# Squares of the last attention's queries on ScalarE, and 64 bytes of padding in SBUF

## The chip, the core and the metric

The kernel runs on one core of a Trainium2 chip. The metric is the device time of one execution in microseconds. Before the change it is 1250.59 us, the median of three runs (1250.11 to 1250.6).

## What is computed

Two transformer blocks in a row on 256 tokens of width 1024, in float32. The first block mixes with a spatial gate, a forgetting attention and a cross attention, and has a feed-forward part with 4096 inner columns (squared ReLU). The second has two layers; each is a SwiGLU feed-forward part of 2816 inner columns, an attention, and another such part: a sliding-window attention in the first layer, a latent attention in the second. The change touches the latent attention:

```python
q = (rmsnorm_2(c_q, q_norm) @ w_uq).reshape(B, S, B_HEADS, dqk)      # 16 heads of 96
k = jnp.concatenate([k_nope, broadcast(k_rope)], axis=-1)
q = rmsnorm_2(q, q_gain); k = rmsnorm_2(k, k_gain)
q = concat(q[..., :64], apply_rope(q[..., 64:], pos))
s = einsum('bqhd,bshd->bhqs', q_blk, k) * dqk**-0.5;  p = softmax(causal(s));  o = p @ v
```

The norm of `q` needs, for each token and head, the sum of the squares of 96 numbers.

## The kernel before

**Products.** The weights come from HBM in pieces (`Stream`, L73): a tile `raw`, three of them in turn, is cast by ScalarE to `wh` in the format fp32r (L103), and VectorE writes the remainder `wl` = `raw` − `wh` (L113); six pairs of `wh` and `wl` are in turn. The low part of a piece also issues the next DMA, on SP's queue. Activations are held as such pairs too: `xh`, `xl` for the residual stream, `ah`, `al` for the inner columns of a feed-forward part, `oh`, `ol` for the attentions' output, `ch`, `cl` for the latent vectors, `mh`, `ml` for the memory. A product is three matmuls: high by high, low by high, high by low. In `mm_t` (L130, matmuls at L135 to L137) the weights are the held operand and 256 columns of activations are streamed; in `mm_n` (L139, L145 to L147) and `mm_y` (L149, L159 to L161) the activations are held and 256 to 512 columns of weights streamed. In a row of the trace the streamed operand is named first.

**Stages, in us from the start of the span.** First block: mixing to 137, feed-forward to 311 (its second product, by `mm_y` with `ah` and `al` held, from 225). Four SwiGLU parts (`ffn2`, L399): gate and up 332 to 447, 589 to 714, 777 to 901 and 1057 to 1181, streaming `xh`, `xl`; down projections 447 to 510, 714 to 777, 901 to 964 and 1181 to the end, streaming `ah`, `al`. Sliding-window attention 510 to 589, latent attention 964 to 1057; both end in an output product that streams `oh`, `ol`. The order of the instructions on each engine is the order of the program text.

**Places in SBUF.** Pools lie one behind another in the order of L54 to L61, then the pools of each stage; each tile is rounded up to 32 bytes a partition. A tile `fill` of 32 bytes (L172), read by nothing, stands ahead of the pool `res`. This gives, in bytes past a multiple of 512: `raw`, `wh`, `wl` 224; `x`, `xh`, `xl` and all tiles of the pool `tp` 0; `kon`, with the identity, 0; and, behind the small tiles of `sm`, every large tile of the stages (`ah`, `al`, `oh`, `ol`, `ch`, `cl`, `mh`, `ml`, the attentions' operands) 480, or 224 in two small pools. All columns and slices that a product takes of `xh`, `ah` or `wh` begin at multiples of 128 bytes within the tile, save the ones of 390 columns.

**The latent attention.** Heads go through a pipe (`Pipe`, L348): `step()` computes the scores of the next heads on TensorE, the transposes of the head two before, masks and takes the maximum on VectorE (`s`, `mx`, `nm`), scales the previous head's `p` by its reciprocal sum on VectorE (L299), and takes the exponential on ScalarE (L281). Queries come in four batches of four heads. `q_mm(b)` is the product, copied to `qn` by ScalarE; `q_sq(b)` squares it into `qsq`, two tiles of 128 x 384; `q_norm(b)` sums the squares on VectorE and takes the power on GpSimd (`rqb`, L198); `q_rope(b)` turns the last 32 columns, on VectorE for batches 0 and 1, on GpSimd for 2 and 3, eight instructions (L1240 to L1245); `head(h)` transposes keys and queries of one head. `k_rstd`, `k_scale` do the keys' norm, `v_mm` the values' product. `q_sq` squares batch 0 on ScalarE and batches 1 to 3 on GpSimd (L1218 to L1225).

Of the kernel before, what the change touches and what calls it, by code (L numbers as in the profile page):

```python
# [9 lines left out]
F32 = mybir.dt.float32  # L10
# [3 lines left out]
AF = mybir.ActivationFunctionType  # L14
ALU = mybir.AluOpType
AX = mybir.AxisListType

P = 128
# [33 lines left out]
def block_kernel(ctx: ExitStack, tc: tile.TileContext, a: dict, out: bass.AP, upto: int = 99):  # L52
# [7 lines left out]
    cst = pool("cst", 1)  # L60
# [3 lines left out]
    act, dve, gp, pe = nc.scalar, nc.vector, nc.gpsimd, nc.tensor  # L64

    def bank():
        return psp.tile([P, 512], F32, tag="ps", name="ps")
# [71 lines left out]
    def mm_n(ps, w, off, n, x, tt, kts, first, last):  # L139
        h, lo = w  # L140
        ts = slice(tt * P, tt * P + P)
        for j, (k, kk) in enumerate(kts):
            c = off + kk * n
            s0, s1 = first and j == 0, last and j == len(kts) - 1
            pe.matmul(ps, lhsT=x[0][k][:, ts], rhs=h[:, c:c + n], start=s0, stop=False)  # L145
            pe.matmul(ps, lhsT=x[1][k][:, ts], rhs=h[:, c:c + n], start=False, stop=False)  # L146
            pe.matmul(ps, lhsT=x[0][k][:, ts], rhs=lo[:, c:c + n], start=False, stop=s1)  # L147
# [33 lines left out]
    cols = cst.tile([P, N_COLS], F32, name="cols")  # L181
    rows = cst.tile([P, N_ROWS], F32, name="rows")
    posn = cst.tile([P, 2], I32, name="posn")
    gp.memset(mhalf, -0.5)
    ident = kon[:, K_ID:K_ID + P]
    uone = kon[:, K_U:K_U + 2 * P]
# [448 lines left out]
    with ExitStack() as es:  # L635
# [51 lines left out]
        for tt in range(2):  # L687
            dve.scalar_tensor_tensor(out=z[:, tt], in0=pf[tt][:, 384:390], scalar=rs_x[:, tt:tt + 1],
                                     in1=rows[:, R_FORGET:R_FORGET + 6], op0=ALU.mult, op1=ALU.add)
# [67 lines left out]
        pipe = Pipe(pp, oh, ol)  # L757
# [194 lines left out]
    with ExitStack() as es:  # L952
# [44 lines left out]
        for tt in range(2):  # L997
            sq = tp.tile([P, T], F32, tag="sq", name="sq")
# [30 lines left out]
        pipe = Pipe(pp, oh, ol)  # L1029
# [81 lines left out]
    with ExitStack() as es:  # L1111
# [7 lines left out]
        qn = [mp.tile([P, 16, 96], F32, name=f"qn{i}") for i in range(2)]  # L1119
# [75 lines left out]
        def k_rstd(nb, ksn):  # L1195
            rks[nb] = rk = sm.tile([P, 2, 8], F32, tag="rk", bufs=2, name="rk")
            rstd_pow(rk.rearrange("p a b -> p (a b)"), ksn.rearrange("p a b -> p (a b)"), 16)
# [13 lines left out]
        def q_mm(b):  # L1211
            w = ws.get()
            for tt in range(2):
                p = bank()
                mm_n(p[:, :384], w, 0, 384, CQ, tt, [(0, 0), (1, 1)], True, True)
                act.copy(qn[tt][:, 4 * b:4 * b + 4, :].rearrange("p h d -> p (h d)"), p[:, :384])

        def q_sq(b):  # L1218
            qq[b] = [pp.tile([P, 4, 96], F32, tag="qsq", bufs=4, name="qsq") for _ in range(2)]
            for tt, sq in enumerate(qq[b]):  # L1220
                qh = qn[tt][:, 4 * b:4 * b + 4, :]
                if b:
                    gp.tensor_tensor(out=sq, in0=qh, in1=qh, op=ALU.mult)
                else:
                    act.activation(out=sq, in_=qh, func=AF.Square)  # L1225

        def q_norm(b):
            for tt in range(2):
# [6 lines left out]
        def q_rope(b, eng=dve):  # L1235
            qr = [qn[tt][:, 4 * b:4 * b + 4, 64:96] for tt in range(2)]
            t = [pp.tile([P, 4, 32], F32, tag="rt", bufs=2, name="rt") for _ in range(2)]
            for lo, hi in ((0, 16), (16, 0)):
                for tt in range(2):
                    eng.tensor_tensor(out=t[tt][:, :, lo:lo + 16], in0=qr[tt][:, :, hi:hi + 16],  # L1240
                                      in1=tq[:, 1, tt][:, None, lo:lo + 16].to_broadcast([P, 4, 16]), op=ALU.mult)
            for tt in range(2):
                eng.tensor_tensor(out=qr[tt], in0=qr[tt], in1=tq[:, 0, tt][:, None, :].to_broadcast([P, 4, 32]), op=ALU.mult)
            for tt in range(2):
                eng.tensor_tensor(out=qr[tt], in0=qr[tt], in1=t[tt], op=ALU.add)  # L1245
# [17 lines left out]
        pipe = Pipe(pp, oh, ol)  # L1263

        def head(h, eng=dve):
            pt = bank()
            for tt in range(2):
                pe.transpose(pt[0:96, tt * P:tt * P + P], kc[tt][:, h, :], ident)
            for tt in range(2):
                pe.transpose(pt[0:96, T + tt * P:T + tt * P + P], qn[tt][:, h, :], ident)  # L1270
            kt_ = pp.tile([96, T], F32, tag="kT", bufs=4, name="kT")
            qt_ = pp.tile([96, T], F32, tag="qT", bufs=4, name="qT")
            (act.copy if eng is act else dve.tensor_copy)(kt_, pt[0:96, 0:T])
            act.activation(out=qt_, in_=pt[0:96, T:], func=AF.Copy, scale=gb[0:96])
            pipe.add(dict(q=qt_, k=kt_, v=[vb[0][:, 64 * h:64 * h + 64], vb[1][:, 64 * h:64 * h + 64]],
                          w=(P, T), front=front_mla, o=h,
                          scale=[rqb[:, h // 4, 0, h % 4:h % 4 + 1], rqb[:, h // 4, 1, h % 4:h % 4 + 1]]))
# [3 lines left out]
        def v_mm(nb):  # L1281
            w = ws.get()
            for tt in range(2):
                p = bank()
                mm_n(p[:, :512], w, 0, 512, CK, tt, [(0, 0)], True, True)
                act.activation(out=vb[tt][:, 512 * nb:512 * nb + 512], in_=p, func=AF.Copy, scale=rv[:, tt:tt + 1])
# [16 lines left out]
        q_mm(0)  # L1303
        psq = colsum(cacc, csq)
        q_sq(0)
        dve.scalar_tensor_tensor(out=eq, in0=psq[:, 0:2], scalar=1.0 / 256, in1=ex, op0=ALU.mult, op1=ALU.add)
        dve.tensor_scalar(out=eq, in0=eq, scalar1=EPS, scalar2=None, op0=ALU.mult)
# [2 lines left out]
        q_mm(1)  # L1310
        q_norm(0)
        head(0, act)
        q_sq(1)
        q_mm(2)
        q_sq(2)
        head(1, act)
        head(2, act)
        pipe.step()
        k_rstd(1, ks1)
        head(3, act)  # L1320
        q_rope(1)
        v_mm(1)
        pipe.step()
        pipe.step()
        head(4)
        q_norm(1)
# [175 lines left out]
```

## Time and profile before

| | |
|---|---|
| median of three runs | 1250.59 us |
| the profiled execution | 1250.49 us |
| its span, first to last instruction | 1248.7 us |
| TensorE busy, matmuls | 9850 matmuls, 98% of the span |
| VectorE, ScalarE, GpSimd busy | 67%, 53%, 14% |
[...]
| read from HBM | 208.71 MB, 168 GB/s over the span |

Busy time counts an instruction from its start to its end; matmuls overlap, so a window full of them says nothing of their pace, and the number of records in it does. "Idle before" is the time for which the engine had nothing under way ahead of an instruction, with what ended it.

### The profile page before, as it was taken

To read this page: it belongs to the slowest core of one execution; us is meant where nothing else is said; L and a number is where in the kernel's file an instruction comes from. 1 tells how busy PE (TensorE), PEld (TensorE's weight loads), DVE (VectorE), ACT (ScalarE), POOL (GpSimd) and SP (SyncE) were. 2 spreads that over 40 slices of the span, in tenths; PEclk is the share of its full clock that TensorE was granted. 3 is DMA by queue.
4 is the path that set the end of the run, shared out by engine and by line. 5 is a ranking of instruction groups with operands and counts; after the bars stand their busy time and mean duration, and the time that the engine had idled before them with its cause. 6 is when DMAs were issued, how large, how long until landed. Compare 5 with 4: busy or idle time off the path is not lost.

```text
span 1248.7 us, 23875 instructions
## 1 busy us (share of the span) xinstructions
PE 1222.7 (98%) x9850; PEld 1169.1 (94%) x9850; DVE 836.3 (67%) x1470; ACT 658.8 (53%) x1164; POOL 171.6 (14%) x168
## 2 busy tenths in 40 slices
PE   8998999999999999999999999999999899999998
PEld 6886999888999999988999999999999779999998
DVE  5867776844688666797666666676666797566653
ACT  5574655443554444587454444444444787454532
POOL 5404100300301001212000011000011552000000
PEclk9999999999999999999999999999999989999999
DMA  7543354655254545623455456455455413455462
GB/s 242 200 141 120 130 208 174 234 204 196 75 203 169 181 147 184 233 102 111 168 195 188 143 185 228 173 187 196 146 186 198 169 36 124 161 189 197 137 212 97
DMA packets 37262, 211.31 MB, mean 169 GB/s; under 512 B 4768, under 2 KB 8224, under 8 KB 18848
## 3 DMA queue, kind: packets, MB, share of 16 engines
q1 hardware_dynamic: 37152, 209.78, 48.4%
q8 instruction: 77, 1.26, 0.4%
q14 instruction: 33, 0.27, 0.1%
HBM read 208.71 MB, written 1.05 MB: 168 GB/s over the span
## 4 chain that ended last, share of the span: by engine, by line
PE 84%; DVE 10%; ACT 3%; issue 1%; DMA 1%; POOL 1%; SPq 0%; ACTq 0%; DVEq 0%; POOLq 0%
PE ps L135 23%; PE ps L136 23%; PE ps L137 23%; DVE wl L113 4%; PE ps L161 3%; PE ps L159 3%; PE ps L160 3%; PE ps L343 1%; PE ps L311 1%; PE ps L145 1%; PE ps L147 1%; PE ps L322 1%; PE ps L146 1%; ACT wh L103 1%; DVE p L299 1%
## 5 line engine op out<-in xcount | busy, mean ns | idle before, releaser
L113 DVE TENSOR_TENSOR wl<-raw,wh 128x1024 fp32r<-128x1024 f32 (+4 forms) x436 | 493.0, 1170 | 54.5 <-ACT wh L103 54.2
L135 PE MATMUL ps<-xh,wh 128*128 128x256 f32 (+1 forms) x1848 | 519.9, 281 | 2.2 <-DVE y L527 1.7
L137 PE MATMUL ps<-xh,wl 128*128 128x256 f32 (+1 forms) x1848 | 516.2, 279 | 1.3 <-DVE wl L113 1.3
L136 PE MATMUL ps<-xl,wh 128*128 128x256 f32 (+1 forms) x1848 | 515.9, 279 | 0.3 <-DVE xl L271 0.3
L103 ACT CAST wh<-raw 128x1024 fp32r<-128x1024 f32 (+4 forms) x436 | 400.8, 958 | 94.0 <-PE ps L160 33.9
L135 PEld LDWEIGHTS ps<-xh,wh 128*128 128x128 f32 (+1 forms) x1848 | 346.7, 188 | 5.0 <-ACT sq L208 2.1
L137 PEld LDWEIGHTS ps<-xh,wl 128*128 128x128 f32 (+1 forms) x1848 | 346.6, 188 | 1.8 <-DVE wl L113 1.7
L136 PEld LDWEIGHTS ps<-xl,wh 128*128 128x128 f32 (+1 forms) x1848 | 346.8, 188 | 0.7 <-DVE xl L271 0.5
L135 PE MATMUL ps<-ah,wh 128*128 128x256 f32 x704 | 199.2, 283 | 0.0
L136 PE MATMUL ps<-al,wh 128*128 128x256 f32 x704 | 199.2, 283 | 0.0
L137 PE MATMUL ps<-ah,wl 128*128 128x256 f32 x704 | 199.2, 283 | 0.0
L409 ACT ACTIVATE s<-t 128x256 f32<-128x256 f32 x88 | 36.9, 420 | 187.5 <-DVE t L407 187.5
L137 PEld LDWEIGHTS ps<-ah,wl 128*128 128x128 f32 x704 | 135.2, 192 | 0.0
L136 PEld LDWEIGHTS ps<-al,wh 128*128 128x128 f32 x704 | 135.1, 192 | 0.0
L135 PEld LDWEIGHTS ps<-ah,wh 128*128 128x128 f32 x704 | 135.1, 192 | 0.0
L209 POOL TENSOR_TENSOR acc<-acc,sq 128x256 f32<-128x256 f32 x49 | 54.8, 1119 | 522.2 <-ACT sq L208 521.8
L262 ACT ACTIVATE xh<-x,cols 128x256 fp32r<-128x256 f32 x56 | 28.5, 510 | 111.1 <-DVE x L455 99.1
L223 DVE TENSOR_TENSOR al<-f,ah 128x256 fp32r<-128x256 f32 (+1 forms) x104 | 48.9, 470 | 52.7 <-ACT ah L222 52.7
L407 DVE TENSOR_TENSOR t<-ps,rb 128x256 f32<-128x256 f32 x88 | 37.2, 423 | 69.8 <-PE ps L137 63.1
L222 ACT CAST ah<-f 128x256 fp32r<-128x256 f32 (+1 forms) x104 | 45.8, 440 | 56.6 <-DVE f L411 43.3
L454 DVE SCALAR_TENSOR_TENSOR t<-ps,rb 128x256 f32<-128x256 f32 x32 | 13.6, 425 | 84.4 <-PE ps L137 84.4
L411 DVE TENSOR_TENSOR f<-ps,s 128x256 f32<-128x256 f32 x88 | 37.4, 426 | 47.6 <-ACT s L409 47.6
(270 smaller groups left out, 1411.6 us busy)
## 6 DMA issues: line engine op xcount, KB each, us to landing
raw<-in_gu SPq DMA_DIRECT2D x88, 1024.0 KB, 4.8
raw<-in_dn SPq DMA_DIRECT2D x64, 704.0 KB, 4.4
raw<-in_ff SPq DMA_DIRECT2D x32, 1024.0 KB, 4.9
raw<-in_w_out SPq DMA_DIRECT2D x4, 1024.0 KB, 4.9
raw<-in_aq SPq DMA_DIRECT2D x4, 1024.0 KB, 4.9
raw<-in_a_out SPq DMA_DIRECT2D x4, 1024.0 KB, 5.3
raw<-in_b_out SPq DMA_DIRECT2D x4, 1024.0 KB, 5.1
raw<-in_w1q SPq DMA_DIRECT2D x6, 512.0 KB, 4.4
```

The lines of the kernel that those rows point to most:

```text
L103: act.copy(h[:, :n], t)
L113: eng.tensor_tensor(out=lo, in0=t, in1=h.bitcast(F32), op=ALU.subtract)
L135: pe.matmul(ps, lhsT=h[:, c:c + m], rhs=x[0][k], start=s0, stop=False)
L136: pe.matmul(ps, lhsT=h[:, c:c + m], rhs=x[1][k], start=False, stop=False)
L137: pe.matmul(ps, lhsT=lo[:, c:c + m], rhs=x[0][k], start=False, stop=s1)
L159: pe.matmul(ps, lhsT=x[0][k][:, ts], rhs=h[:, c:c + n], start=s0, stop=False)
L160: pe.matmul(ps, lhsT=x[1][k][:, ts], rhs=h[:, c:c + n], start=False, stop=False)
L161: pe.matmul(ps, lhsT=x[0][k][:, ts], rhs=lo[:, c:c + n], start=False, stop=s1)
L209: gp.tensor_tensor(out=acc, in0=acc, in1=sq, op=ALU.add)
L222: act.copy(h, src)
L223: dve.tensor_tensor(out=lo, in0=src, in1=h.bitcast(F32), op=ALU.subtract)
L411: dve.tensor_tensor(out=f, in0=u, in1=s, op=ALU.mult)
```

## The change

A tile of 64 bytes is added at the end of the pool `cst`. Nothing reads or writes it. Everything allocated behind it, the pool `sm` and the pools of all stages, lies 64 bytes further on: the tiles that began 480 bytes past a multiple of 512 begin 32 past one, those at 224 begin at 288. `raw`, `wh`, `wl`, `x`, `xh`, `xl`, `tp` and the tiles of `cst` stay.

`q_sq` runs on ScalarE for all four batches. In the order of the program the squares of batches 1 and 2 move behind `head(3)`, with a step of the pipe between them, `v_mm(1)` comes before `q_rope(1)`, and `q_rope(1)` comes a step later.

```diff
@@ -181,6 +181,7 @@
     cols = cst.tile([P, N_COLS], F32, name="cols")
     rows = cst.tile([P, N_ROWS], F32, name="rows")
     posn = cst.tile([P, 2], I32, name="posn")
+    cst.tile([P, 16], F32, name="rest")
     gp.memset(mhalf, -0.5)
@@ -1218,11 +1219,7 @@
             qq[b] = [pp.tile([P, 4, 96], F32, tag="qsq", bufs=4, name="qsq") for _ in range(2)]
             for tt, sq in enumerate(qq[b]):
-                qh = qn[tt][:, 4 * b:4 * b + 4, :]
-                if b:
-                    gp.tensor_tensor(out=sq, in0=qh, in1=qh, op=ALU.mult)
-                else:
-                    act.activation(out=sq, in_=qh, func=AF.Square)
+                act.activation(out=sq, in_=qn[tt][:, 4 * b:4 * b + 4, :], func=AF.Square)
@@ -1310,17 +1307,17 @@
         q_mm(1)
         q_norm(0)
         head(0, act)
-        q_sq(1)
         q_mm(2)
-        q_sq(2)
         head(1, act)
         head(2, act)
         pipe.step()
         k_rstd(1, ks1)
         head(3, act)
+        v_mm(1)
+        q_sq(1)
+        pipe.step()
         q_rope(1)
-        v_mm(1)
-        pipe.step()
+        q_sq(2)
         pipe.step()
         head(4)
         q_norm(1)
```

## Rows read from the trace of the kernel before

**Rows 1.** The page: busy time by engine; chain that ended last.

```profile
PE 1222.7 (98%) x9850; PEld 1169.1 (94%) x9850; DVE 836.3 (67%) x1470; ACT 658.8 (53%) x1164; POOL 171.6 (14%) x168
...
PE 84%; DVE 10%; ACT 3%; issue 1%; DMA 1%; POOL 1%; SPq 0%; ACTq 0%; DVEq 0%; POOLq 0%
```

**Rows 2.** Windows: stretch, length, busy us (records) by engine, PEclk, DMA share.

```profile
394.00:444.00 50.00, 50.00 (x431) 50.00 (x430) 33.11 (x49) 24.75 (x38) 0.00 (x0) 1.00 0.52 183
450.00:500.00 50.00, 50.00 (x419) 50.00 (x418) 32.30 (x46) 23.72 (x39) 6.38 (x5) 1.00 0.55 181
232.00:282.00 50.00, 50.00 (x223) 41.40 (x222) 32.12 (x28) 20.21 (x23) 6.93 (x5) 1.00 0.65 231
```

**Rows 3.** All instructions by form: busy us, mean ns, idle before them.

```profile
L137 PE MATMUL ps<-xh,wl 128*128 128x256 f32 x1840 | 513.9, 279 | 1.3 <-DVE wl L113 1.3
...
L135 PE MATMUL ps<-ah,wh 128*128 128x256 f32 x704 | 199.2, 283 | 0.0
...
L159 PE MATMUL ps<-wh,ah 128*128 128x512 f32 x128 | 49.8, 389 | 0.0
...
L223 DVE TENSOR_TENSOR al<-f,ah 128x256 fp32r<-128x256 f32 x88 | 37.5, 426 | 41.7 <-ACT ah L222 41.7
...
L407 DVE TENSOR_TENSOR t<-ps,rb 128x256 f32<-128x256 f32 x88 | 37.2, 423 | 69.8 <-PE ps L137 63.1 <-ACT rb L255 6.7
...
L136 PE MATMUL ps<-ol,wh 128*128 128x256 f32 x128 | 36.3, 284 | 0.7 <-DVE ol L346 0.7
...
L146 PE MATMUL ps<-wh,ml 128*128 128x256 f32 x16 | 4.5, 283 | 0.0
...
L146 PE MATMUL ps<-wh,xl 128*128 128x256 f32 x16 | 4.5, 281 | 0.0
```

**Rows 4.** Windows of the two output products that stream `oh` and `ol`.

```profile
1029.00:1057.20 28.20, 28.20 (x237) 26.69 (x236) 20.30 (x52) 21.58 (x46) 7.33 (x6) 1.00 0.26 90
558.00:589.00 31.00, 30.27 (x251) 27.69 (x252) 25.38 (x71) 24.10 (x60) 7.74 (x7) 1.00 0.31 104
```

**Rows 5.** Timeline of GpSimd, latent attention: start, length, instruction, idle before.

```profile
993.03 4.23 POOL L1223 TENSOR_TENSOR qsq<-qn 128x384 f32<-128x384 f32 x4
...
1010.30 2.06 POOL L1223 TENSOR_TENSOR qsq<-qn 128x384 f32<-128x384 f32 x2
1012.31 1.20 POOL L1240 TENSOR_TENSOR rt<-qn,tq 128x64 f32<-128x64 f32 x4
```

**Rows 6.** Timeline of VectorE in the same stretch.

```profile
986.95 0.62 DVE L1240 TENSOR_TENSOR rt<-qn,tq 128x64 f32<-128x64 f32 x4
...
994.92 2.59 DVE L1240 TENSOR_TENSOR rt<-qn,tq 128x64 f32<-128x64 f32 x4
...
999.01 0.55 DVE L299 TENSOR_SCALAR p<-p,rd 128x128 f32<-128x128 f32 x2
...
1011.55 1.23 DVE L299 TENSOR_SCALAR p<-p,rd 128x128 f32<-128x128 f32 x2
...
1013.88 1.04 DVE L299 TENSOR_SCALAR p<-p,rd 128x128 f32<-128x128 f32 x2
```

**Rows 7.** Timeline of TensorE in the same stretch.

```profile
999.44 0.87 PE L322 MATMUL ps<-kon,p 128*128 128x128 f32 x3 [2.76 <-DVE p L299]
```

**Rows 8.** Timeline of ScalarE in the same stretch.

```profile
985.52 0.97 ACT L1225 ACTIVATE qsq<-qn 128x384 f32<-128x384 f32 x2
...
999.12 0.49 ACT L281 ACTIVATE p<-s,nm,rqb 128x128 f32<-128x128 f32 x1 [1.33 <-DVE nm L1260]
...
1001.47 0.49 ACT L281 ACTIVATE p<-s,nm,rqb 128x128 f32<-128x128 f32 x1 [0.65 <-DVE nm L1260]
...
1011.73 0.49 ACT L281 ACTIVATE p<-s,nm,rqb 128x128 f32<-128x128 f32 x1 [1.63 <-DVE nm L1260]
```

**Rows 9.** Windows with the lower granted clock.

```profile
999.30:1002.70 3.40, 3.26 (x13) 3.23 (x14) 3.40 (x13) 2.70 (x10) 0.81 (x1) 0.50 0.02 5
1013.00:1016.40 3.40, 3.40 (x18) 2.30 (x18) 3.00 (x12) 2.86 (x10) 2.52 (x7) 0.50 0.00 0
```

## The prediction

> **What bounds the kernel now.** I read the page first: engine shares, then the chain that ended last. TensorE is busy 1222.7 us of a span of 1248.7, and the chain runs through it for 84% [rows 1]. So a change pays where it shortens TensorE's instructions or its gaps; time taken off another engine pays only beside such a gap. The busy share doesn't say how fast TensorE goes while it is busy, so next I read windows of equal length inside stretches without a gap. In 50 us of a gate-and-up stage, where `xh` and `xl` are streamed, 431 matmul records stand; in 50 us of the down projections, where `ah` and `al` are streamed, 419 [rows 2]. A window also catches the two or three records that are still under way at its start (a record lasts 279 to 283 ns, [rows 3]): 50 us / (431 − 2.4) = 116.7 ns from start to start, 50 us / (419 − 2.4) = 120.0 ns. [...] The groups by form show the same gap of 2 to 5 ns in the mean record: 279 with `xh` streamed, 283 and 284 with `ah` and `ol`, and, with the weights streamed and the activations held, 281 against `xl`, 283 against `ml` [rows 3]. The columns of VectorE, ScalarE and DMA don't explain it: the two windows are loaded alike, VectorE 32.30 us of 50 against 33.11, DMA 181 GB/s against 183 [rows 2].
>
> What does differ is the place in SBUF. `x`, `xh`, `xl` start at multiples of 512 bytes; `wh` and `wl` 224 past; everything behind the pool `sm` 480 past. In steps of 128 bytes, weights and later tiles both start 96 past, `xh` at 0. The pairs (0 with 96) and (96 with 0) are the quicker ones, (96 with 96) the slow one. The pad makes the last pair (32 with 96).
>
> **The pad: nothing executed, all later tiles 64 bytes up.** Matmuls with a later tile as an operand, by counts [rows 3]: 704 × 3 = 2112 in the down projections, 128 × 3 = 384 with `oh`, `ol` streamed, 128 × 3 = 384 of 512 columns with `ah`, `al` held in the first block's second feed-forward product. The 2112 and the 512-column ones lie in stretches where TensorE is busy without a gap (50.00 of 50.00 us [rows 2]), the `oh` ones in two stretches where it is busy 28.20 of 28.20 and 30.27 of 31.00 us [rows 4]; some 2880 are thus on the path. (`ch`, `mh` and 96 with `oh` held stand among gaps: counted as nothing, at most 0.6 us.) If the pair (32 with 96) goes at the pace of `xh`, each saves 3.33 ns: 2880 × 3.33 = 9.6 us. What could take the room: in the down stage VectorE is busy 32.30 us of 50, ScalarE 23.72, the DMA engines 0.55 [rows 2]; the gate-and-up stage lives with the quicker pace at 33.11 and 0.52, so nothing comes late.
>
> No row shows 32 with 96, so the price needs both ends. [...] The step between the two known placements is 3.33 ns; an unknown one as far off again on either side gives 113.3 ns (−19.2 us) or 123.3 ns (+9.6 us). Between them: 0 (still the slow class) and −9.6. I take −9.6: of the three known pairs the one whose two tiles have the same remainder by 128 is slow, both pairs with different remainders are quicker, and after the pad the remainders differ. VectorE and ScalarE pay nothing either way: the difference `al`<-`f`,`ah` takes 426 ns with operands at 480, the product `t`<-`ps`,`rb` 423 with operands at 0 [rows 3].
>
> [...]
>
> **The squares.** Six of eight leave GpSimd. Before, four run there as one block of 4.23 us at 993.03 and two of 2.06 us at 1010.30 [rows 5]. VectorE beside them is stretched: the four rope products that take 0.62 us at 986.95 take 2.59 at 994.92, and two scalings of `p` that take 0.55 take 1.23 and 1.04 [rows 6]. Behind the rope stands head 0's scaling of `p`, and TensorE waits 2.76 us for it at 999.44 [rows 7]. After the change the rope comes behind that scaling and nothing squares beside it: 1.97 us less on VectorE, and the wait as it stands goes.
>
> But ScalarE takes what GpSimd gives: 0.97 us for two squares [rows 8], so 1.94 us between 994 and 1004 and 0.97 near 1010. Queued behind them on ScalarE are the exponentials of heads 1 and 2, the copy of `pt` and the next weights' cast. ScalarE's own idle time there is 1.33 us at 999.12 and 0.65 at 1001.47 [rows 8], 1.98 together: the cover is just used up and ScalarE, not VectorE, is late next. So the first four squares gain between 0 and 2.76 us; I take 0.5, near the end that ScalarE sets. The last two fall into a ScalarE wait of 1.63 us at 1011.73 [rows 8]: free. There VectorE gains between 0 and (1.23 + 1.04 − 2 × 0.55) = 1.2 us, for GpSimd's next rope, at 1012.31 [rows 5], moves into the freed place and stretches VectorE in turn; I take 0.8, as the block that goes is the one that stretched it most. [...] Together −2.0 us; the ends are +1.9 (ScalarE's four squares without cover, nothing gained) and −5.7 (2.76 + 1.2 + 1.7). Moving `v_mm(1)` ahead of the rope also moves its cast, its low part on VectorE and the next weights' DMA on SP's queue forward by a few us; the cover is that DMA moves 5 GB/s and less in the next stretch [rows 9], so it costs nothing. `k_rstd(1)` on GpSimd starts up to 4.23 us sooner; only `k_scale(1)`, four heads on, reads it. The squares of batches 1 and 2 now come later in the program, still ahead of the `q_norm(1)` and `q_norm(2)` that read them.
>
> **Sum.** The profiled execution took 1250.49 us (span 1248.7 and 1.8 around it), 0.10 under the median of 1250.59. 1250.49 − 9.6 − 2.0 = 1238.9 us.
>
> **Rivals.**
> - *The address has no part, or 32 is in the same class as 480* (say because what counts is the remainder by 64, which stays 32). Down projections stay at 419 records, only the squares remain: 1250.49 − 2.0 = 1248.5, from 1246 to 1251. For it: no row with this placement. Against it: one shape at two paces, and the pace goes with the tile, not with the load of the other engines. [...]
> - *The pad is worse* (the other side). [...] It decides from the point where the start-to-start time of the down projections exceeds 120.7 ns (2 us eaten by 2880 × 0.7 ns); at 123.3 it costs 9.6: 1250.49 + 9.6 − 2.0 = 1258.1. Against it: the slow pair known is the one with equal remainders.
> - *The pad is better than `xh`'s place*: 113.3 ns, as far from equal remainders as 128 bytes allow. 1250.49 − 19.2 − 2.0 = 1229.3.
> - *The squares do not help*, ScalarE being full: 1.9 us the wrong way; it shifts each case and is in their ranges.
>
> **Chances.** Forecast 0.50 (own range 1235 to 1241.5), no effect of the pad 0.32, worse 0.11, better 0.07. Within 1232 to 1250.5 lie the first nearly whole, four fifths of the second, and little else: 0.49 + 0.27 + 0.02, about 0.8. A measurement of this kernel tells 0.2%, 2.5 us, from no change. Faster: 0.50 + 0.07 + 0.4 × 0.32 = 0.70; the no-effect case leaves 0.18 within and 0.01 slower, the worse case 0.01 within and 0.10 slower: 0.70, 0.19, 0.11.
>
> **What will show it.** 431 records in 50 us of the down projections say the pad works as reckoned, 419 that it does nothing, about 407 that it harms, 443 that it beats `xh`'s place; the gate-and-up stage stays at 431 in all. In the last attention: no squares on GpSimd, the four rope products of batch 1 near 0.6 us, the 2.76 us wait gone, ScalarE without idle time between 994 and 1004, and the scalings of `p` near 0.55 except beside GpSimd's ropes. Wrong would be a gain that sits elsewhere than in the down projections and this one stage.

## The result, and the profile after

The changed kernel took 1236.72 us (median of 4 runs, 1235.40 to 1239.55) against 1250.35 (1248.68 to 1250.60) for the kernel before: a ratio of 0.9894, 95% interval [0.9882, 0.9906]. Measured again it took 1238.60 us (6 runs, 1235.26 to 1242.75) against 1250.68: 0.9903 [0.9884, 0.9921]. 1238.9 was forecast. The total is right; several of its terms are not, and that their errors cancel is luck.

The page of the kernel after, busy time by engine and the chain that ended last:

```profile
PE 1209.8 (98%) x9850; PEld 1154.6 (93%) x9850; DVE 832.2 (67%) x1470; ACT 658.7 (53%) x1170; POOL 167.9 (14%) x162
...
PE 85%; DVE 9%; ACT 3%; issue 1%; POOL 0%; DMA 0%; SPq 0%; DVEq 0%; ACTq 0%; POOLq 0%
```

Against [rows 1] TensorE's busy time fell by 12.9 us, most of the 13.8 us by which the span fell; six instructions moved from GpSimd (168 to 162) to ScalarE (1164 to 1170). Where the span went is read from the start of the first matmul of each stage in the timelines of the two profiled executions:

| stretch | before, us | after, us | difference |
|---|---|---|---|
| start to the first block's feed-forward | 132.91 | 131.27 | −1.64 |
| its second product, 512 columns, `ah`, `al` held | 92.34 | 94.86 | +2.52 |
| down projections, first SwiGLU part | 63.35 | 62.19 | −1.16 |
| second, third, fourth (to the end of the span) | 63.36, 63.35, 67.35 | 59.84, 59.85, 63.82 | −3.52, −3.50, −3.53 |
| latent attention | 92.57 | 89.85 | −2.72 |
| all the rest together | 673.5 | 673.2 | −0.25 |

The windows of the kernel after answer to [rows 2] and [rows 4]: down projections of the first and second part, the 512-column product, the sliding attention's output product, and gate-and-up of the second part.

```profile
450.00:500.00 50.00, 50.00 (x426) 50.00 (x426) 33.15 (x47) 24.51 (x40) 6.36 (x5) 1.00 0.55 182
716.00:766.00 50.00, 50.00 (x444) 50.00 (x443) 33.16 (x47) 23.36 (x40) 6.38 (x5) 1.00 0.60 201
232.00:282.00 50.00, 50.00 (x216) 40.26 (x216) 29.31 (x27) 20.28 (x23) 7.53 (x4) 1.00 0.62 229
558.00:589.00 31.00, 30.18 (x255) 27.59 (x254) 25.34 (x69) 24.20 (x59) 8.06 (x7) 1.00 0.31 107
620.00:670.00 50.00, 50.00 (x431) 50.00 (x430) 31.76 (x45) 24.35 (x36) 0.00 (x0) 1.00 0.53 188
```

The down projections went from 419 records to 426 in the first part and 444 in the second (the third and fourth have 443 and 444 too); gate-and-up stayed at 431; the 512-column product fell from 223 to 216. The start times of the matmuls in the timeline give the paces, from the start of one matmul to the start of the next, more finely, and they are constant through a stretch: before 120.0 ns in all down projections and in the output products with `oh`; after 117.8 in the first down projections and with `oh`, 113.3 in the other three; in the 512-column product 226.7 before, 233.3 after. Below, a pace is told so, with the count of its window beside it: 443 or 444 is 113.3 ns, 431 is 116.7, 426 or 427 is 117.8, 419 is 120.0. The forms of the kernel after show the same in the mean length of a record, against 279, 283, 389 and 284 in [rows 3]:

```profile
L137 PE MATMUL ps<-xh,wl 128*128 128x256 f32 x1840 | 513.8, 279 | 1.2 <-DVE wl L113 1.2
...
L135 PE MATMUL ps<-ah,wh 128*128 128x256 f32 x704 | 195.0, 277 | 0.0
...
L159 PE MATMUL ps<-wh,ah 128*128 128x512 f32 x128 | 50.6, 396 | 0.0
...
L136 PE MATMUL ps<-ol,wh 128*128 128x256 f32 x128 | 35.9, 280 | 0.8 <-DVE ol L347 0.8
```

**The latent attention.** It lies 7.45 us earlier than before. The timeline of GpSimd has no squares. Between the power for the keys' norm, which ends at 988.5, and the next row it is idle; four squares ran ahead of that power before [rows 5]:

```profile
994.23 1.64 POOL L199 TENSOR_TENSOR rqb<-rqb,mhalf 128x8 f32<-128x8 f32 x1 [5.75 <-DVE rqb L1227]
```

VectorE's rope products of batch 1 take 0.63 us where they took 2.59, and the scalings of `p` 0.55 except beside GpSimd's ropes (0.68 to 0.82, where two took 1.23 and 1.04) [rows 6]:

```profile
989.95 0.63 DVE L1237 TENSOR_TENSOR rt<-qn,tq 128x64 f32<-128x64 f32 x4
...
994.82 0.55 DVE L300 TENSOR_SCALAR p<-p,rd 128x128 f32<-128x128 f32 x2
...
998.84 0.82 DVE L300 TENSOR_SCALAR p<-p,rd 128x128 f32<-128x128 f32 x2
...
1002.68 0.68 DVE L300 TENSOR_SCALAR p<-p,rd 128x128 f32<-128x128 f32 x2
...
1004.36 0.82 DVE L300 TENSOR_SCALAR p<-p,rd 128x128 f32<-128x128 f32 x2
```

ScalarE has no idle time over 0.3 us from 986.7 to 1001.6; the squares of batches 1 and 2 stand in it:

```profile
989.82 0.93 ACT L1222 ACTIVATE qsq<-qn 128x384 f32<-128x384 f32 x2
...
991.71 0.94 ACT L1222 ACTIVATE qsq<-qn 128x384 f32<-128x384 f32 x2
...
997.00 0.48 ACT L326 COPY pt<-ps 128x384 f32<-128x384 f32 x1 [0.24 <-PE ps L323]
...
1002.85 0.49 ACT L282 ACTIVATE p<-s,nm,rqb 128x128 f32<-128x128 f32 x1 [1.25 <-DVE nm L1257]
```

TensorE no longer waits 2.76 us for head 0's `p` [rows 7]. A shorter wait has come, for batch 1's rope. VectorE itself waited 0.45 us for ScalarE's cast before it; the rest is VectorE's own work, the low part and the rope:

```profile
991.34 0.52 PE L1267 MATMUL ps<-kon,qn 128*96 128x128 f32 x2 [1.92 <-DVE qn L1242]
...
988.80 1.23 DVE L113 TENSOR_TENSOR wl<-raw,wh 128x1024 fp32r<-128x1024 f32 x1 [0.45 <-ACT wh L103]
```

Of the two stretches at clock 0.50 [rows 9] one is left, here:

```profile
992.70:996.10 3.40, 3.40 (x15) 3.25 (x14) 3.32 (x13) 3.40 (x10) 1.87 (x2) 0.50 0.00 0
```

### The profile page after: what moved, and what is told of

Read it like the earlier page. It is cut to its first block, busy times and chain, and to the rows that moved or that the text cites. A ratio compares the mean times of both kernels' runs of the same rounds, so it can differ in the third digit from the quotient of the medians.

```text
span 1234.9 us, 23880 instructions
## 1 busy us (share of the span) xinstructions
PE 1209.8 (98%) x9850; PEld 1154.6 (93%) x9850; DVE 832.2 (67%) x1470; ACT 658.7 (53%) x1170; POOL 167.9 (14%) x162
## 4 chain that ended last, share of the span: by engine, by line
PE 85%; DVE 9%; ACT 3%; issue 1%; POOL 0%; DMA 0%; SPq 0%; DVEq 0%; ACTq 0%; POOLq 0%
PE ps L135 23%; PE ps L136 23%; PE ps L137 23%; DVE wl L113 4%; PE ps L161 3%; PE ps L159 3%; PE ps L160 3%; PE ps L312 1%; PE ps L344 1%; PE ps L323 1%; PE ps L145 1%; PE ps L147 1%; PE ps L146 1%; ACT p L282 1%; ACT ah L223 0%
## 5 line engine op out<-in xcount | busy, mean ns | idle before, releaser
L135 PE MATMUL ps<-ah,wh 128*128 128x256 f32 x704 | 195.0, 277 | 0.0
L136 PE MATMUL ps<-al,wh 128*128 128x256 f32 x704 | 194.8, 277 | 0.0
L137 PE MATMUL ps<-ah,wl 128*128 128x256 f32 x704 | 194.8, 277 | 0.0
L137 PEld LDWEIGHTS ps<-ah,wl 128*128 128x128 f32 x704 | 132.2, 188 | 0.0
L135 PEld LDWEIGHTS ps<-ah,wh 128*128 128x128 f32 x704 | 132.1, 188 | 0.0
L136 PEld LDWEIGHTS ps<-al,wh 128*128 128x128 f32 x704 | 132.0, 188 | 0.0
```

The source lines that it names most:

```text
L135: pe.matmul(ps, lhsT=h[:, c:c + m], rhs=x[0][k], start=s0, stop=False)
L136: pe.matmul(ps, lhsT=h[:, c:c + m], rhs=x[1][k], start=False, stop=False)
L137: pe.matmul(ps, lhsT=lo[:, c:c + m], rhs=x[0][k], start=False, stop=s1)
```

## The experiments

Each short diff is against the kernel named beside it; the hunks are shortened, and remarks behind `#` are this text's.

**The two parts alone.** `pad_only` is the kernel before with the line of the pad; `squares_only` is the kernel after without it.

```diff
+    cst.tile([P, 16], F32, name="rest")     # pad_only: this line alone
```

> The kernel before plus the 64 bytes alone; the squares stay on GpSimd. My theory (the pad carries most of the gain, through the pace of the matmuls that stream a later tile): the down projections go as in the changed kernel, 113.3 ns from start to start in three of them and 117.8 in the first, the 512-column products with activations held at 233.3 ns instead of 226.7, and the time is 1250.4 - 11.7 - 0.6 + 2.5 - about 0.5 = about 1240 us. Rival (the pace comes from the moved squares or from the state of the chip): the down projections at 120.0 ns and about 1250 us.

> The changed kernel without the 64 bytes. My theory: down projections at 120.0 ns as before, the latent attention shorter by about 2 us (its stage from first projection to next feed-forward part went from 92.6 to 89.9 us, and some 0.4 of that is the pace of its output product), so about 1248 us. Rival (ScalarE full, the squares give nothing by themselves): 1250 us or above.

The pad alone: 1239.28 us (4 runs), 0.9908 [0.9889, 0.9927]. The squares alone: 1248.30 (10 runs), 0.9982 [0.9973, 0.9992]. The product of the two ratios is 0.9890, the change's 0.9894: within these intervals the two effects add up. Windows of the pad alone, 512-column product and the first and second part's down projections:

```profile
232.00:282.00 50.00, 50.00 (x216) 40.30 (x216) 31.33 (x28) 19.99 (x22) 7.82 (x5) 1.00 0.64 231
450.00:500.00 50.00, 50.00 (x427) 50.00 (x426) 31.99 (x47) 23.98 (x41) 6.27 (x5) 1.00 0.54 182
716.00:766.00 50.00, 50.00 (x444) 50.00 (x443) 33.89 (x49) 24.88 (x42) 6.37 (x5) 1.00 0.57 187
```

The counts are the changed kernel's. With the squares alone the same windows show those of before:

```profile
232.00:282.00 50.00, 50.00 (x223) 41.41 (x222) 31.22 (x28) 20.51 (x23) 7.79 (x5) 1.00 0.64 231
450.00:500.00 50.00, 50.00 (x419) 50.00 (x418) 32.27 (x45) 23.38 (x39) 6.37 (x5) 1.00 0.57 184
```

Its latent attention takes 90.09 us against 92.57, 2.48 less, and TensorE's row there has the same new wait:

```profile
999.45 0.52 PE L1266 MATMUL ps<-kon,qn 128*96 128x128 f32 x2 [1.94 <-DVE qn L1241]
```

**Other sizes of the pad.** The kernel after with 32, 96 and 128 bytes in place of 64. The later tiles then lie 0, 64 and 96 bytes past multiples of 512.

```diff
-    cst.tile([P, 16], F32, name="rest")
+    cst.tile([P, 8], F32, name="rest")      # pad32; pad96: [P, 24]; pad128: [P, 32]
```

> The changed kernel with 32 bytes of padding in place of 64: later tiles at multiples of 512, as xh is. Theory of places (what counts is where the streamed tile and the held one start, by 128 bytes): down projections at 116.7 ns like the stages that stream xh, all four of them alike, so about 7.0 us less than at 120.0; the 512-column products with a held tile at 0 near the 226.7 of before or a little less; about 1241 us. Theory of 64-byte halves (only the remainder by 64 counts, and 32 and 96 are one class): the change's gain came from something else, and this one, at 0, is the odd one out: another pace than 113.3 or 117.8 in any case.

> The changed kernel with 96 bytes: later tiles 64 past a multiple of 512. Theory of places by 128 bytes, with the price set by the distance of the two remainders round a circle of 128: distance 32, as for xh (0 with 96), so 116.7 to 118 ns, about 1241 us. If the price falls with the order (streamed ahead of held or behind it): 113.3 or 120, 1237 or 1248 us. The 512-column products with the activations held show the same question the other way round: 226.7 if only equal remainders are quick there, 233.3 if the later tile's own place counts.

> The kernel after with a pad of 128 bytes in place of 64: the later tiles lie 96 bytes past multiples of 512, so their remainder by 128 is that of the kernel before (96) and of the hot weights (224 by 256), but not their remainder by 256 (96 against 224). If remainders by 128 set the pace: down projections 120.0 ns and the 512-column stage 226.7 ns, as before, and 1248.3 us with the squares' gain. If 256 counts: the 512-column stage near the 232.4 ns of the kernel with such places, +2 us, and the down projections elsewhere between 113 and 118 ns, so 1233 to 1246 us.

`pad32`: 1242.72 us, 0.9939 [0.9922, 0.9955]; every down projection at 116.7 ns, the pace of `xh`, whose place the tiles then share; the 512-column product slow:

```profile
232.00:282.00 50.00, 50.00 (x216) 40.27 (x215) 30.00 (x28) 20.16 (x23) 9.79 (x4) 1.00 0.64 229
450.00:500.00 50.00, 50.00 (x431) 50.00 (x430) 33.48 (x47) 24.40 (x41) 6.37 (x5) 1.00 0.55 183
```

`pad96`: 1250.92 us, 1.0008 [0.9999, 1.0018], with the squares' gain in it; down projections at 120.0 although the remainders by 128, 64 and 96, differ. It is 2.6 us slower than `squares_only`, and its 512-column product, at 234.3 ns, accounts for that: 384 × 7.6 ns = 2.9 us.

```profile
232.00:282.00 50.00, 50.00 (x215) 40.17 (x214) 30.58 (x27) 19.98 (x22) 10.51 (x5) 1.00 0.65 231
450.00:500.00 50.00, 50.00 (x419) 50.00 (x418) 30.94 (x46) 23.04 (x39) 5.23 (x5) 1.00 0.56 183
```

`pad128`, one execution: 1248.62 us. Its remainders by 128 are those of before (96 with 96), its paces are not: 118.7 ns (424) for 120.0, and 233.3 (216) for 226.7. The down projections lie outside both ranges that were expected.

```profile
232.00:282.00 50.00, 50.00 (x216) 40.25 (x215) 30.08 (x28) 19.95 (x22) 8.20 (x5) 1.00 0.65 231
450.00:500.00 50.00, 50.00 (x424) 50.00 (x423) 31.78 (x47) 23.91 (x41) 6.14 (x5) 1.00 0.53 179
```

So in these runs the pace went with the place: 116.7, 113.3 or 117.8, 120.0 and 118.7 ns in the down projections with pads of 32, 64, 96 and 128 bytes. The remainder by 128 alone does not describe it: with equal ones there are 120.0 ns before and 118.7 in `pad128`.

**The weights moved instead of the later tiles.** `wp_moved` is `squares_only` with `raw`, `wh` and `wl` 64 bytes on (288 past multiples of 512); `xh` stays at 0, the later tiles at 480.

```diff
-    mhalf = lead.tile([P, 24], F32, name="mhalf")
-    lead2.tile([P, 8], F32, name="fill")
+    mhalf = lead.tile([P, 40], F32, name="mhalf")
+    lead2.tile([P, 120], F32, name="fill")
```

> The changed kernel without its 64 bytes; instead the weights' pool alone lies 64 bytes further on (wh, wl at 32 by 128 in place of 96), with filler so that xh stays at 0 and the later tiles at 96. Theory of differences (what counts is the streamed tile's place less the held one's, round 128: 0 gave 120.0 ns, 32 gave 116.7, 64 gave 113.3 or 117.8, 96 gave 120.0): the gate-and-up stages, 0 less 32 = 96, go from 116.7 to 120.0; the down projections, 96 less 32 = 64, from 120.0 to 113.3 or 117.8; the 512-column products, 32 less 96 = 64, from 226.7 to 233.3; time about 1248.3 + 18 - 11 + 2.5 = 1258 us. Theory of the streamed tile's own place (0 gives 116.7, 32 gives 113.3 or 117.8, 64 and 96 give 120.0, wherever the weights lie): nothing changes there, 116.7 and 120.0, and about 1248 us.

1246.82 us (5 runs), 0.9972 [0.9953, 0.9992]. Windows of the 512-column product, the first and second down projections, and gate-and-up:

```profile
232.00:282.00 50.00, 50.00 (x221) 41.00 (x220) 32.37 (x29) 20.40 (x23) 9.35 (x5) 1.00 0.65 231
450.00:500.00 50.00, 50.00 (x443) 50.00 (x442) 33.56 (x48) 24.94 (x42) 6.36 (x5) 1.00 0.57 186
716.00:766.00 50.00, 50.00 (x427) 50.00 (x426) 32.56 (x47) 24.68 (x42) 6.38 (x5) 1.00 0.53 176
620.00:670.00 50.00, 50.00 (x425) 50.00 (x424) 31.35 (x44) 24.14 (x35) 0.00 (x0) 1.00 0.52 180
```

The weights' place counted here as well: with it alone moved, gate-and-up slowed to 118.3 ns (425) and the down projections quickened to 113.3 (443) and 117.8 (427). Neither theory on record holds: by the one of differences gate-and-up would be at 120.0, the 512-column product at 233.3 (it is at 228.9, 221 records) and the total at 1258 us; by the other nothing would have moved. And the same two paces, 113.3 and 117.8, came in the opposite order: now the first part is the quick one.

**Is the first part slow by its addresses?** `dn1_high` is the kernel after with a hole of 32 KiB in the second part's pool, so that its `ah` and `al` lie where the first part's do.

```diff
         with tc.tile_pool(name="ffa", bufs=1) as fa, tc.tile_pool(name="fft", bufs=2) as ft:
+            if high:                            # second SwiGLU part only
+                fa.tile([P, 8192], F32, name="hole")
```

> The changed kernel with the second feed-forward part's tiles 32 KiB higher, at exactly the addresses that the first one has, where the down projections went at 117.8 ns and not at 113.3. Theory of the address (which 32 KiB the tiles lie in sets which of the two paces it is): the second down projection at 117.8, about 2.4 us more. Theory of the entry (two paces are possible at the same place, and how a stretch is entered picks one, which then holds to its end): it stays at 113.3, no change in the time, or changes for a reason that the addresses do not give.

One execution: 1238.01 us, first part 426 records, second 443, as without the hole. With the same addresses the two stages run at different paces, 117.8 and 113.3 ns.

```profile
450.00:500.00 50.00, 50.00 (x426) 50.00 (x426) 32.15 (x47) 24.49 (x41) 6.36 (x5) 1.00 0.53 178
716.00:766.00 50.00, 50.00 (x443) 50.00 (x442) 34.08 (x48) 24.48 (x42) 6.38 (x5) 1.00 0.57 188
```

**Stops inside the stretches.** `kick_mid` is the kernel after with tiny matmuls ahead of the third, fifth and seventh output tile of each down projection; their result is read by nobody.

```diff
                 p = bank()
+                if d == 2 or d == 4:
+                    for i in range(d // 2):
+                        pe.matmul(p[:, T:T + 1], lhsT=ident, rhs=ones[:, 0:1], start=True, stop=True)
+                elif d == 6:
+                    pe.matmul(p[:, T:T + 64], lhsT=ident, rhs=ident[:, :64], start=True, stop=True)
```

> The kernel after, with small extra matmuls between the output tiles of each down projection, in a spare part of the bank: one of one column ahead of the third output tile, two of one column ahead of the fifth, one of 64 columns ahead of the seventh (their result is read by nobody). Addresses, weights and order stay. If the pace of a down projection (117.78 ns in the first, 113.33 in the other three) is picked by how the stretch is entered and then held, some of these twelve disturbances change it: parts of the first at 113.33 ns or parts of the others at 117.78, each part steady to its end, and the time moves by +-0.3 us for each changed part of 132 matmuls (132 x 4.45 ns = 0.59 us at most). If the pace belongs to the stage (its weights' places in the ring, its transfers), every part of the first stays at 117.78 and every part of the others at 113.33, whatever the disturbance, and the time is that of the kernel after plus 16 small matmuls, about 2 us at most.

One execution: 1247.52 us. Windows of 13 us, the first three in the first part (before the first disturbance, behind it, behind the second), the last two in the second part (before and behind the first):

```profile
451.00:464.00 13.00, 13.00 (x117) 13.00 (x116) 8.63 (x14) 7.09 (x12) 0.00 (x0) 1.00 0.52 172
467.00:480.00 13.00, 13.00 (x113) 13.00 (x112) 9.34 (x12) 6.76 (x12) 2.15 (x2) 1.00 0.55 177
483.00:496.00 13.00, 13.00 (x113) 13.00 (x112) 9.15 (x12) 6.54 (x11) 2.81 (x2) 1.00 0.53 176
717.00:730.00 13.00, 13.00 (x117) 13.00 (x117) 8.60 (x13) 6.95 (x12) 0.00 (x0) 1.00 0.51 174
733.00:746.00 13.00, 13.00 (x113) 13.00 (x112) 9.11 (x12) 6.49 (x11) 2.14 (x2) 1.00 0.55 177
```

By the windows' own arithmetic 117 records in 13 us are 113.3 ns and 113 are 117.8. All twelve parts behind a disturbance run at 117.8 to their end, whatever its kind; all four ahead of the first run at 113.3, in the first part too, which had 117.8 at the same addresses in the kernel after. So in this execution each of the 16 parts held one pace, and the only change, from 113.3 ns to 117.8, came at the first disturbance of each stage. The cost is there as well: a down projection with its three stops takes 62.50 us in the second part, against 59.84: 396 × 4.44 ns = 1.8 us for the pace and 0.9 for the stops themselves. Over the four stages it is 8.3 us, more than was expected: every first disturbance led from the quicker pace to the slower, and the stops cost 3.6 us where 2 at most was expected.

This execution shows a third pace with `xh` streamed at 0 and the weights at 224. In the first part 288 matmuls of gate-and-up, where nothing was changed, ran at 120.0 ns; the kernel after had 116.7 there. The first row is this run, the second the kernel after:

```profile
340.00:370.00 30.00, 30.00 (x253) 30.00 (x252) 22.46 (x37) 15.70 (x25) 0.00 (x0) 1.00 0.44 152
```

```profile
338.00:368.00 30.00, 30.00 (x260) 30.00 (x259) 22.48 (x36) 15.70 (x26) 0.00 (x0) 1.00 0.45 156
```

**The pad without the 512-column product.** `stage_pad` leaves the first block's tiles where they were and puts the 64 bytes at the head of the later pools. `res32` moves `xh` too (fill of 64 bytes, so 32 past multiples of 512; the later stages' tiles at 32, the first block's at 96), to see gate-and-up at that place.

```diff
-    cst.tile([P, 16], F32, name="rest")
         with tc.tile_pool(name="ffa", bufs=1) as fa, tc.tile_pool(name="fft", bufs=2) as ft:
+            fa.tile([P, 16], F32, name="rest")
...
+        mp.tile([P, 16], F32, name="rest")   # first in the pools of both attentions
```

> A version meant to beat both: the 64 bytes stand at the head of the four SwiGLU parts' pool and of the two later attentions' pools, not ahead of the first block's, so that the products of 512 columns that hold oh or ah keep their old place. Expected: 226.7 ns there instead of 233.3 (384 x 6.6 = 2.5 us, and 0.5 for the 96 in the output product), all else as in the changed kernel: 1236.7 - 3.0 = 1233.7 us. If the places of the held tiles have no part in it: 1236.7.

> As the last one, and in addition x, xh, xl at 32 by 128 instead of 0, with the later tiles still at 32 and the first block's at 96. Both theories of places put the stages that stream xh into the class that gave 113.3 or 117.8 ns. If 113.3 is the rule there: 5300 x 3.3 = 17.5 us less, about 1216 us; if 117.8: 5.9 us more, about 1240 us; a mixture by stages lies between. If the quick pace belongs to the down projections alone: 116.7 and 1234 us.

`stage_pad`: 1235.90 us (4 runs), 0.9882 [0.9868, 0.9897]. Its 512-column product is back at 226.7 ns:

```profile
232.00:282.00 50.00, 50.00 (x222) 41.42 (x221) 32.68 (x29) 19.92 (x22) 7.48 (x5) 1.00 0.67 231
...
397.00:447.00 50.00, 50.00 (x427) 50.00 (x426) 32.56 (x47) 23.48 (x36) 0.00 (x0) 1.00 0.51 172
```

but the second row is its first gate-and-up stage, at 117.8 instead of 116.7, with nothing moved there; 1233.7 us was expected. `res32`: 1249.18 us (10 runs), 0.9986 [0.9976, 0.9996]; all gate-and-up and all down projections at 117.8, and the 512-column product at 232.4 (217). For gate-and-up at 117.8 some 1240 us was expected; the three down projections that had 113.3 (3 × 528 × 4.44 ns = 7.0 us) and the 512-column product (384 × 5.6 = 2.2) are the rest. Streamed at 32 with the weights at 224, three down projections of the kernel after had 113.3 ns; gate-and-up at that place has 117.8, against 116.7 at 0.

**The two best, side by side, and how one program varies.** The kernel after and `stage_pad` once more, on one chip.

> The kernel after once more, beside the kernel with the pad only at the head of the later pools, on one chip. If the 512-column stage costs it 2.5 us (233.3 for 226.7 ns in 384 matmuls), it takes 1237 us, 2 to 3 us more than the other. If the paces that each execution picks (117.78 or 113.33 in the first down projection, 116.67 or 117.78 in gate-and-up) outweigh that, the two are within 1 us of each other and their executions spread over 3 us or more.

> The pad at the head of the later pools alone, the first block's tiles where they were. If its 512-column stage (226.7 ns) is worth its 2.5 us in every execution: 1234 to 1235 us, below every execution of the kernel after. If its first block's gate-and-up stretches run at 117.8 ns as in its first profile (1.1 ns x some 1500 matmuls = 1.7 us): 1236 us, not told from the kernel after.

1238.60 us (6 runs, 1235.26 to 1242.75) and 1239.02 (6 runs, 1233.56 to 1240.69): not told apart; the 2.5 us of the 512-column product are inside the spread. The kernel before, beside them, spreads from 1249.04 to 1251.70. The profiled execution of the kernel after, 1240.73 us this time, shows one reason why it spreads more (gate-and-up and down projections of the second part, down projections of the third):

```profile
620.00:670.00 50.00, 50.00 (x427) 50.00 (x426) 31.58 (x45) 24.17 (x35) 0.00 (x0) 1.00 0.52 183
716.00:766.00 50.00, 50.00 (x427) 50.00 (x426) 32.70 (x47) 24.72 (x41) 6.37 (x5) 1.00 0.55 178
905.00:955.00 50.00, 50.00 (x443) 50.00 (x443) 32.87 (x47) 22.61 (x39) 6.37 (x5) 1.00 0.63 204
```

The same program had 431 and 444 in the first two of these. The difference is worth 960 × 1.11 + 528 × 4.44 ns = 3.4 us, and the first part's gate-and-up, also at 117.8 this time, adds 768 × 1.11 = 0.9; the two profiled executions differ by 4.0. Over the seven profiled kernels with the weights at 224, `xh` at 0 and these tiles at 32, 28 down projections were entered: 6 behind a gate-and-up stretch that ended at 117.8 ns, all 6 at 117.8; 22 behind one at 116.7, 20 of them at 113.3. The four of `res32`, with `xh` at 32, also came behind 117.8 and ran at 117.8.

## Why the prediction was right, point by point

- **TensorE's pace depends on where its operands lie: right**, and shown by pads alone, which execute nothing. The first rival (no effect, 1248.5 us) is out. For this one shape, 256 streamed columns at a granted clock of 1.00, the runs have 113.3 to 120.0 ns, by place; the pad alone (`pad_only`) took the down projections from 120.0 ns (419) to 117.8 in the first part (427) and 113.3 in the second (444).
- **"The pace of `xh`", one pace for the pair: the term was mis-sized**, −7.0 us for 2112 matmuls of the down projections. They gave −11.7 (the table): three stages took the pace of the rival "better than `xh`'s place", 113.3 ns, one took 117.8, and none 116.7. What stood in the place of a pace for each pair is two paces, 113.3 and 117.8 ns, one of them all through a stage.
- **The same pace for 384 matmuls of 512 columns: wrong in sign.** −1.3 us forecast, +2.5 measured, 384 × 6.6 ns. The price had been carried over from 256 streamed columns of activations to 512 streamed columns of weights; the window of that product [rows 2], 223 records, showed a pace of its own, and no other placement of it was known. `stage_pad`, which leaves these tiles alone, keeps 226.7. The matmuls with `oh` held, counted as nothing, show the same sign: of 60 in a row, those without a stop between went from 228 ns to 234.
- **The output products with `oh`, `ol`**: −1.3 forecast, 117.8 ns measured: 264 matmuls that run without a stop × 2.2 = −0.6.
- **The reason, equal remainders by 128 slow, different ones quick: fell.** `pad96` has different remainders and 120.0 ns, `pad128` has those of before and other paces. That the 9.6 us came out (−11.7 + 2.5 − 0.6 = −9.8 in this execution) is luck: the down projections gave 4.7 us more than forecast, the 512-column product 3.8 and the output products 0.7 less. The forecast total stood on a supposed reason that fell and on a price from one form that was put on another.
- **The squares: right in size and mostly in mechanism.** −2.0 forecast; the latent attention gave −2.72, of which some 0.3 are the `oh` products, and `squares_only` gave 0.9982 [0.9973, 0.9992], 1.0 to 3.4 us. Against `pad_only`, whose latent attention took 91.82 us, the squares give 1.96 in that stage. The 2.76 us wait went, VectorE's rope is at 0.63, ScalarE is full where it was said, and the two scalings that took 1.23 and 1.04 gave back 0.77 us, 0.8 forecast. That ScalarE would be late next was right only in part: of the new wait of 1.92 us, 0.45 comes from VectorE's wait for ScalarE's cast, and the rest from VectorE's own low part and rope.
- **The clock in that stage: not shown in the size that was put in.** The forecast −2.0 is 0.5 and 0.8 us for the squares and 0.7, of a possible 1.7, for the two stretches of 3.40 us at clock 0.50 [rows 9]; the 0.7 was the author's estimate, and no run shows it. What the traces show is that the second stretch went whole. How many there are varies: the granted clock over the stage is 0.96 in the two traces with the squares on GpSimd (`before`, `pad_only`), and in the twelve with them on ScalarE 0.98 (one stretch left) or 1.00 (none). `dn1_high`, whose latent attention has the changed kernel's instructions and places, has none and takes 89.65 us there against 89.85 (its row below). By these two executions the stretch that was left costs 0.2 us, and not the 1.7 that was reckoned for one in which TensorE is busy throughout, as it is here. What the one that went is worth by itself isn't shown.

```profile
959.00:1048.00 89.00, 82.30 (x615) 72.69 (x614) 71.75 (x235) 76.06 (x190) 35.06 (x43) 1.00 0.29 103
```

- **Outside the forecast: −1.6 us ahead of the first feed-forward.** The stretch with the granted clock at 0.50 near 119 us lasted 6.8 us before and 3.4 after. Here 117 to 127 us, the clock in the third column from the right, before, after, and in `dn1_high`:

```profile
117.00:127.00 10.00, 7.53 (x20) 5.50 (x21) 9.27 (x8) 5.92 (x11) 1.18 (x1) 0.66 0.47 166
```

```profile
117.00:127.00 10.00, 7.91 (x58) 5.90 (x59) 9.02 (x10) 6.34 (x12) 0.80 (x1) 0.83 0.49 177
```

```profile
117.00:127.00 10.00, 7.78 (x20) 5.72 (x21) 9.02 (x8) 5.78 (x10) 0.94 (x1) 0.66 0.47 176
```

It is not the change's: `dn1_high` has the changed kernel's instructions and places up to here, and its feed-forward starts at 132.80 us, as late as before, where the kernel after has 131.27 and, measured again, 131.15. The clock alone does not explain it either: the two profiled executions of `stage_pad`, one program, show 0.66 and 0.83 in this window and start the feed-forward at 132.80 and 133.56.

## What to carry to other kernels

Count the records in equal windows of a stretch where the engine is busy throughout: a pace that differs between two stages of one shape (here 431 records in 50 us against 419) is a place to look, and a cheap probe is a pad that executes nothing (`pad_only`: 1239.28 us against 1250.32). Carry a measured pace only to the same form, streamed and held operand and columns alike, and run pads of several sizes, since what one stream gains another can lose: here 64 bytes gave the down projections −11.7 us and the 512-column product +2.5. Where one program shows two paces from execution to execution (here 431 and 427 records in one window of gate-and-up), compare many runs, and read from a profile which pace each stage had before giving a difference of 1 or 2 us to an edit.

## What was not expected of the hardware

One shape with one set of places ran at several steady paces: 113.3 and 117.8 ns (streamed at 32, weights at 224), or 116.7, 117.8 and, over 288 matmuls of `kick_mid`, 120.0 (streamed at 0). The first four of these were held over 528 to 960 matmuls. Behind the tiny matmuls of `kick_mid` stood the slower of the first two, 117.8 ns, twelve times of twelve, in four of them after 113.3. What makes an undisturbed entry take one or the other (20 of 22 quick behind 116.7) stays open, and so does the form of the dependence on the places. Remainders by 128 do not settle the paces, since 96 and 480, equal by 128, differ (118.7 and 120.0 ns in the down projections); by 256 no two of the places tried are equal, so that stays untested. By the streamed operand's place, weights at 224, the down projections had 116.7 at 0, 113.3 or 117.8 at 32, 120.0 at 64, 118.7 at 96, 120.0 at 480; the 512-column product had 226.7 with the held tiles at 480 and 232.4 to 234.3 at the other four. At 96 it had 233.3 in `pad128` and 232.4 in `res32`, so for it too the places do not settle the pace alone.
